# One load on another queue, three stores halved by columns, and a new order of visits in a seven-product weight gradient

## The chip, the cores and the metric

The kernel runs on one core of a Trainium2 chip. The time is device microseconds (us) of one execution. The engines are TensorE (PE in the profile, its weight loads PEld), VectorE (DVE), ScalarE (ACT), GpSimd (POOL) and SyncE (SP). SP and ACT issue plain DMAs, each on a queue of its own; POOL issues DMAs that also convert f32 to bf16. All of these queues are served by the same 16 DMA engines.

## The reference

```python
batch, m, k, n = 16, 512, 1024, 768          # f32
grad_weight = np.einsum('bmk,bmn->kn', input, grad_output)
return grad_weight.astype(np.float32)        # 1024 x 768
```

It is one matrix product: X (8192 x 1024) transposed, times G (8192 x 768). The sum runs over 8192 rows.

## The kernel before, in words

**Slices and pairs.** The 8192 rows are cut into 64 slices of 128 rows. Two slices make a unit u = 0 to 31. Units 0 to 4 and 31 are worked on as single slices ("s" in `LOADS`, L12): four result blocks A, B, C, D (K halves by N halves), each of four row blocks q of 128, get one matmul per slice. Units 5 to 30 are worked on as pairs ("P"): seven products (A, B, C, 1, 5, 6, 7) take the place of eight, in the manner of Strassen and Winograd. For them DVE makes sums and differences of the halves: `x0.u`, `x1.u`, `x2.u` of X (L195, L197, L199) and `g0.u`, `g1.u`, `g2.u` of G (L205, L207, L209). One block matmul is 128x128 weights against 384 columns.

**Loads.** Slice 0 of both inputs and X of slice 1 come as f32 (tiles `xf` and `gf`, L141 to L144): SP issues the left and then the right 384 columns of G, ACT issues X of slice 0 and then X of slice 1. DVE and ACT round these to bf16 in twelve pieces, `r0` to `r16` in the plan (L216 to L229): r10 and r11 are the left half of G, r0 the right half; r12 to r16 are X of slice 0; r1 to r4 are X of slice 1. Everything else is loaded by POOL straight into bf16: slices of units 0 to 4 one by one (L171, L173), later units whole (L166, L167), into ten buffers for each of X and G.

**Banks and visits.** PSUM has eight banks. A visit "C2@7.3" opens bank 7 for block C, q = 2, and adds three slices or pairs to it; "C2.1" goes on with an open one. Bank numbers 0 to 2 hold the four A blocks, packed, all along; two of these are cut over two banks and so take two matmuls a visit (128 and 256 columns). "c" and "v" close a visit on ACT or DVE: the first time by a copy, later by an add to the sum in SBUF (DVE, L364) or, where "f" had first filled the bank with the old sum (ACT, L292), by a copy back (ACT, L360). "z" puts a bank aside and "y" adds it later (L376, L385). At the end "v" adds a shared product (L357) or, for product 5, subtracts it from two sums (L352, L353), and "w" lets POOL do such an addition in SBUF (L392).

**What sets the order.** `PLAN` (L15 to L76) is a list of some 2,000 tokens written out. It is run through once (L394) and gives PE, DVE, ACT and POOL their instructions in exactly that order: each engine works its own off in order and waits where data, a bank or a buffer is late. POOL's loads stand ahead of its additions; SP's stores follow in the order in which blocks are closed. PE gets 920 block matmuls. `SPARE_LOADS` (L87) adds a second weight load to every other matmul in a range. The last block to close is B3, over two banks: its 256 columns leave by ACT's queue and its 128 by SP's (L366); every other block leaves by SP's (L370).

Of the kernel before, what the change touches and what calls it, by code (L numbers as in the profile page):

```python
# [9 lines left out]
P = 128  # L10
# [2 lines left out]


PLAN = (  # L15
    "r11 r10 r16 r14 r15 A1.1 r13 r12 A0.1 C2@7.1 C0@3.1 A2.1 A3.1 cC0 r0 vC2 D1@6.1 D3@5.1 r4 B2@4.1 r2 "
    "B1@7.1 vD1 r3 B0@3.2 cB2 A0.1 r1 B1.1 vD3 cB0 A2.1 A3.1 D0@6.1 cB1 D0.1 D2@3.2 cD0 D3@7.1 C3@5.2 vD3 "
    "C1@4.2 cC3 C1.1 A1.2 cC1 C0@5.2 cD2 A2.1 D1@4.2 C2@3.2 vD1 B3@7.3 vC2 B3.1 A3.2 vB3 D0@4.2 B1@6.2 vD0 "
    "B2@3.2 zcB1.0 B2.1 A2.1 A0.1 vB2 A0.1 D3@6.2 vC0 D3.1 C1@7.2 C3@5.2 vC1 C3.1 A1.2 vC3 A0.1 B0@3.2 vD3 "
    "B0.2 D2@7.2 vB0 D2.2 C2@5.1 fC3@3 A1.1 vD2 B3@4.2 A0.1 fD2@6 C3.1 vB3 C1@7.1 A2.1 cC3 A2.1 vC1 A0.1 A2.1 "  # L20
    "B3@4.1 D0@3.2 vB3 C2.3 B2@7.3 A3.2 vB2 A3.2 D2.1 vC2 D2.1 C0@7.5 B1@5.2 vC0 B1.2 A0.1 yB1.0 D1@7.6 B1.1 "
    "A0.1 A1.3 D0.3 D3@4.5 B1.1 D0.1 vD3 D2.2 D1.1 vD0 A3.1 cD2 A3.1 vB1 B0@4.1 zcD1.17 B0.2 g0.5 B0.1 B2@3.2 "
    "vB0 B2.1 B3@6.2 g1.5 B3.1 C1@5.1 vB2 C1.3 g2.5 C3@3.1 vB3 C3.3 x0.5 C3.1 C2@6.3 vC3 C2.1 52@4.1 C1.1 "
    "yD1.17 zcC2.5 A0.1 72@3.1 c52 A2.1 x1.5 A2.2 c72 A2.1 g0.6 62@7.1 vC1 A1.2 70@4.1 g1.6 50@3.1 63@5.1 c70 "
    "v62 73@6.1 A0.1 A3.1 g2.6 12@4.1 x2.5 C0@7.2 c12 C0.1 x0.6 C0.1 c50 A2.1 A3.1 f62@4 A0.1 x1.6 73.1 "
    "71@3.1 vC0 71.1 c73 63.1 A1.1 c71 x2.6 62.1 B3@7.1 c63 yC2.5 61@6.2 B3.1 c62 g0.7 B2@3.2 c61 60@5.2 vB2 "
    "B1@4.2 c60 B0@6.1 vB3 B0.1 10@3.2 vB0 11@5.2 g1.7 11.1 10.1 x0.7 13@6.1 c11 13.2 c10 A0.1 g2.7 53@5.1 "
    "vB1 53.1 fC1@3 53.1 70@7.1 x1.7 70.1 c13 A1.1 51@4.1 v70 c53 51.2 C1.1 g0.8 C1.1 c51 A3.1 x2.7 C3@5.1 "
    "cC1 C3.1 72@4.1 g1.8 72.1 vC3 f12@3 52@6.2 A2.1 g2.8 12.1 f71@5 12.1 x0.8 12.1 f60@7 A2.1 A0.1 A1.1 c12 "
    "x1.8 72.1 71.2 v72 f73@3 52.1 60.2 c71 x2.8 73.2 v52 c60 61@4.2 c73 A3.1 g0.9 63@7.1 fC0@5 63.1 v61 "  # L30
    "50@3.2 fB2@6 50.1 v63 C0.1 f10@4 C0.1 B2.1 g1.9 B2.1 B1@7.2 g2.9 cB2 10.1 x0.9 10.1 C0.1 C2@6.1 c10 C2.1 "
    "vB1 C2.2 f62@4 A2.1 x1.9 50.1 f51@7 A3.1 A0.1 x2.9 62.2 v50 62.1 51.1 vC2 51.1 c62 B0@3.2 g0.10 B0.1 "
    "fC1@4 B3@6.2 vB0 c51 B3.1 C1.2 vB3 A1.1 f70@3 13@7.2 x0.10 cC1 13.1 70.2 f11@6 A1.1 v13 70.1 A2.1 g1.10 "
    "11.1 f53@7 11.1 x1.10 11.1 A3.1 c70 g2.10 53.2 x2.10 c11 53.1 71@3.1 g0.11 71.1 c53 61@4.2 v71 B2@6.1 "
    "fC3@7 B2.1 A0.1 v61 60@3.2 vB2 C3.1 f12@4 C3.2 g1.11 C0.1 f63@6 12.1 x0.11 12.2 cC3 63.2 c12 x1.11 A0.1 "
    "A1.1 fB0@7 A3.1 x2.11 60.1 63.1 B0.1 v60 B0.1 c63 A2.1 72@4.1 g2.11 f73@3 72.1 g0.12 72.1 C0.1 cB0 "
    "B1@6.1 v72 B1.2 f10@7 73.1 g1.12 73.2 vB1 11@4.1 10.1 c73 10.1 g2.12 10.1 x0.12 f53@3 C0.1 11.1 50@6.1 "
    "c10 50.1 v11 50.1 53.1 f51@7 53.1 v50 C1@4.2 c53 C1.1 x1.12 A0.1 fB3@6 51.1 g0.13 51.2 52@3.1 vC1 52.1 "
    "c51 52.1 x2.12 52.1 A3.1 fC2@7 g1.13 A2.1 B3.1 v52 f70@4 B3.2 C2.1 g2.13 C2.1 fC3@3 C2.1 x0.13 C2.1 A1.2 "
    "cC2 70.1 x1.13 70.1 cB3 70.1 72@7.1 x2.13 72.1 c70 C3.2 v72 C3.1 61@6.2 g0.14 cC3 61.1 62@4.1 fB2@7 62.1 "  # L40
    "v61 62.2 fB1@3 B2.1 g1.14 B2.2 g2.14 B0@6.2 v62 cB2 A3.1 B1.1 vB0 B1.1 f11@7 C0.2 x0.14 cB1 12@4.3 11.1 "
    "f63@3 11.1 v12 71@6.3 x1.14 f60@4 71.1 63.1 x2.14 63.1 cC0 63.1 v71 A3.1 60.1 c63 60.1 g0.15 60.1 A2.2 "
    "c60 73@6.1 g1.15 73.2 g2.15 53@4.2 v73 13@3.4 f52@6 x0.15 13.1 11.1 zc53.20 C1@5.2 x1.15 c11 C1.1 51@4.2 "
    "vC1 51.1 A1.2 v13 fC2@5 A2.1 52.1 x2.15 52.2 g0.16 50@7.2 c52 50.1 C2.2 v50 B3@3.2 cC2 B3.1 v51 70@6.2 "
    "zcB3.6 g1.16 A0.2 f72@7 x0.16 A0.2 A1.1 A3.1 v70 A3.1 A2.1 72.1 x1.16 f70@6 72.2 x2.16 71@3.2 c72 y53.20 "
    "B0@5.3 v71 70.1 B1@7.2 c70 vB0 B1.1 10@3.1 f63@4 10.1 vB1 10.2 fB2@5 63.1 g0.17 63.1 f13@7 12@6.2 x0.17 "
    "12.1 c63 A3.1 13.2 v12 10.1 A1.1 A0.1 zc10.17 x1.17 B2.2 g2.16 B2.1 g1.17 73@3.2 cB2 g0.18 73.1 62@6.1 "
    "c13 62.1 v73 62.2 61@4.1 g1.18 61.1 fC0@3 61.1 g2.17 61.1 g2.18 f53@5 C3@7.2 v61 C3.2 C0.1 x0.18 C0.3 "
    "C3.1 v62 53.1 cC0 53.2 x1.18 53.1 51@3.1 vC3 51.1 c53 51.1 60@4.1 f50@6 g0.19 60.3 fC2@5 yB3.6 A0.1 A2.1 "
    "f11@7 A2.1 y10.17 A1.1 50.2 x2.18 50.1 C2.1 v60 C2.1 c50 C2.1 11.2 cC2 x0.19 11.2 52@4.2 c11 x1.19 52.2 "  # L50
    "x2.17 70@5.1 fB3@7 70.1 g1.19 70.1 A3.1 x2.19 A3.1 zc70.2 51.1 g0.20 A1.1 f72@6 B3.3 zc52.7 g1.20 B3.1 "
    "g2.19 72.2 cB3 v51 72.1 B1@4.2 c72 g2.20 B1.1 C1@5.2 vB1 C1.3 x0.20 53@7.1 71@3.2 vC1 71.2 A2.2 x1.20 "
    "f62@5 A1.1 53.1 x2.20 B2@4.2 v71 B2.2 B0@6.2 vB2 B0.2 62.1 g0.21 f73@4 62.2 v53 63@3.2 c62 63.1 g1.21 "
    "63.1 f13@7 A3.1 vB0 A3.1 A0.2 y70.2 A0.1 13.2 g2.21 13.1 x0.21 13.1 C0@6.2 c13 C0.1 73.1 x1.21 f61@5 "
    "73.3 x2.21 A2.1 61.1 vC0 c73 61.2 zc63.21 61.1 g0.22 60@6.1 f50@7 60.1 y63.21 60.1 12@4.2 zc60.4 g1.22 "
    "12.2 x0.22 12.1 A0.1 A1.2 v12 72@6.2 x1.22 72.1 50.1 y52.7 50.1 zc72.19 50.2 c61 g2.22 C2@4.1 B1@3.1 "
    "x2.22 51@6.1 f10@5 51.1 g0.23 51.1 C2.1 c50 C2.1 v51 C2.1 B1.2 g1.23 10.2 zcB1.2 g2.23 10.3 x0.23 10.1 "
    "70@7.2 c10 70.1 y72.19 70.1 52@3.2 v70 52.2 A3.1 vC2 A3.1 zc52.9 C3@6.1 x1.23 C3.1 f61@5 C3.2 x2.23 C3.1 "
    "A0.1 B3@4.1 vC3 B3.3 g0.24 61.2 vB3 11@7.2 c61 11.1 x0.24 11.1 fB0@4 11.1 A2.3 v11 71@5.2 x1.24 71.1 "
    "fB2@7 71.1 A0.1 x2.24 A1.1 B0.1 g0.25 B0.3 g1.24 A3.1 62@6.1 g1.25 cB0 62.1 g2.24 62.1 fC1@3 62.1 v71 "  # L60
    "B2.3 v62 B2.1 13@5.2 g2.25 cB2 13.1 x0.25 13.1 f63@6 53@4.4 x1.25 53.1 63.1 y60.4 63.3 v13 63.1 C0@7.2 "
    "g0.26 c63 C0.2 A1.1 f51@6 g1.26 C1.2 y52.9 C1.3 vC0 A0.1 51.1 cC1 51.2 zc53.12 12@5.1 x0.26 12.1 c51 "
    "12.2 A3.1 g2.26 A3.1 60@7.1 x1.26 60.2 v12 60.2 A1.1 yB1.2 A1.1 72@3.2 g0.27 72.2 v60 70@4.3 v72 73@5.1 "
    "f50@7 73.2 g1.27 73.1 f52@3 73.1 x2.26 10@6.2 g2.27 10.2 x0.27 50.3 v73 50.2 A1.1 v70 A2.1 c50 A2.2 "
    "x1.27 52.1 f61@7 52.1 g0.28 52.2 A0.2 g1.28 61.1 x2.25 61.2 x2.27 61.1 C0@5.1 v10 C0.1 c61 B3@4.2 c52 "
    "g2.28 B3.2 B2@6.1 x0.28 B2.2 C0.1 C2@7.1 vB2 C2.3 x1.28 C2.2 vC0 A0.1 A3.2 vB3 fB1@5 63@6.2 g0.29 63.1 "
    "A2.1 62@3.1 v63 62.3 x2.28 B1.1 fC3@6 B1.1 v62 B1.3 g1.29 B1.1 C3.1 g2.29 C3.2 x0.29 C3.3 A2.1 y53.12 "
    "13@4.1 cC3 13.2 x1.29 cB1 13.1 71@6.2 v13 71.3 g0.30 f10@4 C1@5.2 v71 C1.1 zcC2.3 C1.1 11@3.1 x2.29 11.1 "
    "f12@7 11.1 vC1 11.2 10.1 g1.30 12.1 f60@5 12.2 x0.30 12.1 f71@6 11.1 10.1 c12 10.1 v11 A2.1 A1.3 f61@7 "
    "x1.30 13@3.1 c10 A0.1 61.1 v13 61.2 71.1 x2.30 f62@3 60.2 v61 60.1 f72@4 60.1 62.1 v71 f63@7 62.1 72.2 "  # L70
    "g2.30 72.1 f53@6 72.1 v62 63.2 A3.1 v60 f73@3 A3.3 v72 fC0@5 A2.2 v63 73.3 vA3 73.1 f70@7 A1.2 v73 A0.3 "
    "vA2 70.1 f50@3 wC3 70.2 vA1 70.1 53.2 vA0 53.1 wC1 fC3@4 53.2 v70 C0.1 f52@0 C0.2 v53 C0.1 fC1@7 50.3 "
    "fD0@1 C3.2 vC0 C3.1 fB1@6 wD3 C1.2 v50 fD1@2 C1.1 D0.2 f51@5 52.1 wB3 52.1 cC1 52.1 yC2.3 D1.2 v52 51.1 "
    "fD3@7 51.2 cC3 51.2 fD2@3 D3.1 vD0 D3.1 B1.1 fC2@4 B1.1 v51 B1.1 cD3 B1.1 D2.2 C2.1 fB2@7 C2.1 vD2 C2.1 "
    "fB0@1 C2.1 B2.1 vB1 B2.1 fB3@3+0 B2.2 vD1 B2.1 B0.1 vC2 B0.3 vB2 B0.4 B3.2 vB0 B3.3 cB3 "
).split()  # L76


WARMUP = [("b", 512), ("f", 512), ("f", 512), ("b", 512)]
PAIRS_HELD = 10  # L80
SUMS_HELD = 8
ASIDE = 24

MERGED = 5


SPARE_LOADS = range(200, 450)  # L87
PACKED = True
PLACES = {
    0: [(0, 0, 0, 384)],  # L90
    1: [(0, 384, 0, 128), (1, 0, 128, 384)],
    2: [(1, 256, 0, 256), (2, 0, 256, 384)],
    3: [(2, 128, 0, 384)],
}


HALVED = 3


@with_exitstack  # L100
def kernel(
# [6 lines left out]
    nc = tc.nc  # L108
# [11 lines left out]
    X = input.rearrange("b m k -> (b m) k")  # L120
# [20 lines left out]
    nc.sync.dma_start(out=gf[:, LEFT], in_=G[0:P, LEFT])  # L141
    nc.scalar.dma_start(out=xf[0], in_=X[0:P, :])
    nc.sync.dma_start(out=gf[:, RIGHT], in_=G[0:P, RIGHT])
    nc.scalar.dma_start(out=xf[1], in_=X[P : 2 * P, :])  # L144

    wps = psum.tile([P, 512], f32, name="bank7")
    for dt, cols in WARMUP:
# [119 lines left out]
    fresh = {(p, q): True for p in streams for q in range(Q)}  # L267
    closed = set()
    opened = {}
    stored = []  # L270
    used = {7}

    def bank(b):
# [57 lines left out]
    def store(p, q, c0, c1, queue):  # L331
        row = q if p in "AB" else Q + q
        at = (0 if p in "AC" else NH) + c0
        halves = [slice(0, P)]
        if len(stored) < 2 * HALVED:
            halves = [slice(0, P // 2), slice(P // 2, P)]
        for rows in halves:
            stored.append(rows)
            queue.dma_start(out=OUT[rows, row, at : at + c1 - c0], in_=sum_of(p, q)[rows, c0:c1])

    def close(engine, p, q):
        parts, carried = opened.pop((p, q))
# [107 lines left out]
```

## Time and profile before

| | |
|---|---|
| runs shown | 162.37, 162.81, 163.12 us; median 162.81 |
| profiled execution | 162.31 us, its span 160.5 us, clock 1.00 |
| PE busy | 154.8 us, 1007 matmuls (6 of them warm-up) |
| DVE busy | 140.0 us, 323 instructions |
| ACT / POOL busy | 91.5 / 41.9 us |
| PE, first and last matmul of the product | starts at 5.22 us, ends at 156.69 us |
| last load lands / last store lands | 142.69 us / 159.62 us |
| DMA | 33.4 MB, mean 208 GB/s |

The page divides the span into 40 slices of 4 us and gives each engine's busy share in tenths. The timeline lists instructions in the order of time, like ones merged: start, time from the first one's start to the last one's end, engine, line, operation, count, and in brackets the idle time ahead of them and what ended it. A landing time is the moment at which the last of the 16 DMA engines told that its part is done; these times and the single packets are in the trace's DMA records.

### The profile page before, as it was taken

The page shows a single profiled execution, that of the slowest core. Times are in us where ns is not written, and L with a number is a line of the kernel's source. Part 1 is how long each engine was busy: PE and PEld are TensorE (multiplying, and loading weights), DVE is VectorE, ACT ScalarE, POOL GpSimd, SP SyncE. Part 2 cuts the span into 40 slices and gives each one's busy share as a digit, 9 for nine tenths or more (in the row PEclk, how much of TensorE's full clock was granted, in tenths as well). Part 3 has the DMA queues.
Part 4 walks back from the last instruction along what each step waited for, and adds up shares of the span by engine and source line. Part 5 has one row for each costly group of instructions (what it writes and reads, how often), then busy time and mean ns, then how long its engine had stood idle before and what let it go on. Part 6 is the DMA issues. An engine that isn't in the chain of part 4 may idle for free.

```text
span 160.5 us, 2979 instructions
## 1 busy us (share of the span) xinstructions
PE 154.8 (96%) x1007; PEld 99.8 (62%) x1132; DVE 140.0 (87%) x323; ACT 91.5 (57%) x206; POOL 41.9 (26%) x79
## 2 busy tenths in 40 slices
PE   8799999999999999999999999999999999999990
PEld 3266666577777766776665666666666656666560
DVE  0548853999999999999999989999999989999991
ACT  3571301167998888885675774654443423776940
POOL 7445433222212222221222221222222100004400
PEclk9999999999999999999999999999999999999999
DMA  4999999999999999999999999999999999932776
GB/s 168 298 206 210 208 210 216 212 215 213 211 213 213 213 213 212 213 214 215 214 213 212 212 213 212 214 212 212 214 214 212 213 213 214 212 60 67 229 259 231
DMA packets 13310, 33.41 MB, mean 208 GB/s; under 512 B 1520, under 2 KB 5104, under 8 KB 13296
## 3 DMA queue, kind: packets, MB, share of 16 engines
q0 software_dynamic: 10224, 28.64, 90.9%
q1 hardware_dynamic: 2640, 3.41, 6.6%
q10 hardware_dynamic: 432, 1.18, 1.9%
q8 instruction: 8, 0.13, 0.3%
q14 instruction: 6, 0.05, 0.1%
HBM read 58.72 MB, written 3.15 MB: 385 GB/s over the span
## 4 chain that ended last, share of the span: by engine, by line
PE 91%; DMA 3%; DVE 2%; issue 1%; SPq 0%; DVEq 0%
PE bank L321 91%; DMA gf<-in_grad_output_dram 3%; DVE acc L357 1%; DVE macc L353 0%; SPq L141 0%; DVE gp L213 0%; DVE bank L292 0%; DVE macc L352 0%; DVEq L445 0%; DVEq L357 0%; DVEq L362 0%
## 5 line engine op out<-in xcount | busy, mean ns | idle before, releaser
L321 PE MATMUL bank<-gp,xp 128*128 128x384 bf16 (+2 forms) x689 | 110.8, 307 | 1.1 <-DVE gp L213 0.7
L321 PEld LDWEIGHTS <-xp 128*128 128x128 bf16 x689 | 64.5, 98 | 32.8 <-DVE xp L213 1.5
L321 PE MATMUL bank<-ge,xe 128*128 128x384 bf16 x312 | 62.1, 326 | 0.0
L321 PEld LDWEIGHTS <-xe 128*128 128x128 bf16 x312 | 29.9, 97 | 14.2 <-DVE xe L197 0.3
L364 DVE TENSOR_TENSOR acc<-bank,acc 128x384 f32<-128x384 f32 x56 | 29.9, 552 | 9.1 <-PE bank L321 8.7
L360 ACT COPY macc<-bank 128x384 f32<-128x384 f32 x59 | 27.1, 481 | 14.3 <-PE bank L321 13.4
L292 ACT COPY bank<-macc 128x384 f32<-128x384 f32 x56 | 26.7, 484 | 11.3 <-DVE macc L364 6.0
L364 DVE TENSOR_TENSOR macc<-bank,macc 128x384 f32<-128x384 f32 x52 | 28.2, 553 | 0.9 <-PE bank L321 0.4
L360 ACT COPY acc<-bank 128x384 f32<-128x384 f32 (+1 forms) x35 | 16.2, 475 | 17.9 <-PE bank L321 17.6
L167 POOL DMA_DIRECT2D xp<-in_input_dram x27 | 14.3, 530 | 44.6 <-DMA xp<-in_input_dram 19.8
L166 POOL DMA_DIRECT2D gp<-in_grad_output_dram x27 | 14.3, 530 | 36.1 <-PE bank L321 23.6
L292 ACT COPY bank<-acc 128x384 f32<-128x384 f32 (+1 forms) x35 | 16.4, 482 | 9.4 <-DVE acc L364 6.3
L195 DVE TENSOR_TENSOR xe<-xp 128x1024 bf16<-128x1024 bf16 x26 | 17.8, 684 | 0.1
L205 DVE TENSOR_TENSOR ge<-gp 128x768 bf16<-128x768 bf16 x26 | 14.3, 550 | 0.0
L376 ACT COPY aside<-bank 128x384 f32<-128x384 f32 x15 | 7.2, 480 | 8.8 <-PE bank L321 8.6
L197 DVE TENSOR_TENSOR xe<-xe,xp 128x512 bf16<-128x512 bf16 x26 | 10.9, 419 | 0.3
L199 DVE TENSOR_TENSOR xp<-xp,xe 128x512 bf16<-128x512 bf16 x26 | 10.8, 420 | 0.3
L320 PEld LDWEIGHTS <-xp 128*128 128x128 bf16 x76 | 7.4, 98 | 4.6 <-DMA xp<-in_input_dram 0.3
L392 POOL TENSOR_TENSOR acc<-acc,macc 128x384 f32<-128x384 f32 x4 | 3.9, 1000 | 20.7 <-DVE macc L357 19.8
L209 DVE TENSOR_TENSOR gp<-ge,gp 128x384 bf16<-128x384 bf16 x26 | 9.1, 351 | 0.2
L207 DVE TENSOR_TENSOR ge<-gp,ge 128x384 bf16<-128x384 bf16 x26 | 9.0, 351 | 0.1
L320 PEld LDWEIGHTS <-xe 128*128 128x128 bf16 x49 | 4.8, 98 | 2.7
(24 smaller groups left out, 47.4 us busy)
## 6 DMA issues: line engine op xcount, KB each, us to landing
xp<-in_input_dram POOLq DMA_DIRECT2D x27, 512.0 KB, 16.7
gp<-in_grad_output_dram POOLq DMA_DIRECT2D x27, 384.0 KB, 16.7
out_dram<-acc SPq DMA_DIRECT2D x12, 192.0 KB, 2.0
xp<-in_input_dram POOLq DMA_DIRECT2D x8, 256.0 KB, 8.5
gp<-in_grad_output_dram POOLq DMA_DIRECT2D x9, 192.0 KB, 8.5
xf<-in_input_dram ACTq DMA_DIRECT2D x2, 512.0 KB, 5.0
out_dram<-acc SPq DMA_DIRECT2D x6, 96.0 KB, 2.2
gf<-in_grad_output_dram SPq DMA_DIRECT2D x2, 192.0 KB, 4.7
```

The costliest lines, as they stand in the source:

```text
L166: nc.gpsimd.dma_start(out=gp, in_=G[rows, :].rearrange("(p m) n -> p m n", m=2))
L167: nc.gpsimd.dma_start(out=xp, in_=X[rows, :].rearrange("(p m) k -> p m k", m=2))
L195: nc.vector.tensor_sub(out=xe[:, 0:2, :], in0=x[:, 1::-1, :], in1=x[:, 3::-2, :])
L197: nc.vector.tensor_sub(out=xe[:, 2, :], in0=xe[:, 0, :], in1=x[:, 0, :])
L199: nc.vector.tensor_add(out=x[:, 1, :], in0=x[:, 2, :], in1=xe[:, 2, :])
L205: nc.vector.tensor_add(out=ge[:, 0:2, :], in0=g[:, 0:2, :], in1=g[:, 1::2, :])
L209: nc.vector.tensor_add(out=g[:, 1, :], in0=ge[:, 2, :], in1=g[:, 2, :])
L292: copy(out=tile_[:, t0 : t0 + c1 - c0], in_=sum_of(p, q)[:, c0:c1])
L320: nc.tensor.ldweights(stat)
L321: nc.tensor.matmul(tile_[:, t0 : t0 + c1 - c0], stat, mov[:, c0:c1], start=start, stop=True, skip_group_check=True,)
L360: nc.scalar.copy(out=d, in_=b)
L364: nc.vector.tensor_add(out=d, in0=b, in1=d)
```

## The change

X of slice 1 is issued by SP behind the right half of G, instead of by ACT behind X of slice 0. Of the stores, number 0, 1 and 7 are cut into two halves of 192 columns with all 128 partitions; before, the first three were cut into two halves of 64 partitions. `PLAN` is another list: the same 920 block matmuls, the same roundings and sums, in another order, with 146 "v" for 137, 100 "c" for 94, 96 "f" for 91, 9 "z" and 9 "y" for 15 and 15, and 3 "w" for 4. Its last block takes banks 3 and 6 instead of 3 and 0. The range of spare weight loads ends five matmuls later.

```diff
 PLAN = (
-    "r11 r10 r16 r14 r15 A1.1 r13 r12 A0.1 C2@7.1 C0@3.1 A2.1 A3.1 cC0 r0 vC2 D1@6.1 D3@5.1 r4 B2@4.1 r2 "
-    "B1@7.1 vD1 r3 B0@3.2 cB2 A0.1 r1 B1.1 vD3 cB0 A2.1 A3.1 D0@6.1 cB1 D0.1 D2@3.2 cD0 D3@7.1 C3@5.2 vD3 "
...
-    "fD3@7 51.2 cC3 51.2 fD2@3 D3.1 vD0 D3.1 B1.1 fC2@4 B1.1 v51 B1.1 cD3 B1.1 D2.2 C2.1 fB2@7 C2.1 vD2 C2.1 "
-    "fB0@1 C2.1 B2.1 vB1 B2.1 fB3@3+0 B2.2 vD1 B2.1 B0.1 vC2 B0.3 vB2 B0.4 B3.2 vB0 B3.3 cB3 "
+    "r11 r10 r16 r14 A1.1 r13 C3@6.1 r0 r12 A2.1 r15 B3@7.1 cC3 B1@3.1 D0@5.1 cB3 A0.1 vB1 B2@4.1 cD0 A3.1 "
+    "D2@7.1 r1 C1@3.1 r3 r2 D1@6.1 vB2 r4 D3@5.2 D2.1 D1.1 cD3 B0@4.2 cD1 A3.1 C0@5.1 cB0 C0.1 C2@6.2 cD2 "
...
+    "C0.2 v50 fD1@5 C0.1 52.2 cC2 52.1 D1.1 fB2@6 D1.1 v52 B1.2 cD1 B1.1 B2.1 fD0@2 B2.1 vB1 B2.2 fD2@0 B2.1 "
+    "vC0 D0.1 fB0@5 D0.1 D2.1 vB2 D2.1 B0.2 vD2 B0.1 fB3@3+6 B0.2 vD0 B0.2 B3.2 vB0 B3.3 cB3 "
 ).split()
...
-SPARE_LOADS = range(200, 450)
+SPARE_LOADS = range(200, 455)
...
-HALVED = 3
+HALVED = (0, 1, 7)
...
     nc.sync.dma_start(out=gf[:, RIGHT], in_=G[0:P, RIGHT])
-    nc.scalar.dma_start(out=xf[1], in_=X[P : 2 * P, :])
+    nc.sync.dma_start(out=xf[1], in_=X[P : 2 * P, :])
...
-        halves = [slice(0, P)]
-        if len(stored) < 2 * HALVED:
-            halves = [slice(0, P // 2), slice(P // 2, P)]
-        for rows in halves:
-            stored.append(rows)
-            queue.dma_start(out=OUT[rows, row, at : at + c1 - c0], in_=sum_of(p, q)[rows, c0:c1])
+        cuts = [c0, (c0 + c1) // 2, c1] if stored[0] in HALVED else [c0, c1]
+        stored[0] += 1
+        for a, b in zip(cuts, cuts[1:]):
+            queue.dma_start(out=OUT[:, row, at + a - c0 : at + b - c0], in_=sum_of(p, q)[:, a:b])
```

## The prediction

> **What bounds the kernel now.** I read the page first, then the chain of waits, the timeline of the head, of the middle and of the tail, and the busy time by stage.
>
> ```profile
> span 160.5 us, 2979 instructions
> PE 154.8 (96%) x1007; PEld 99.8 (62%) x1132; DVE 140.0 (87%) x323; ACT 91.5 (57%) x206; POOL 41.9 (26%) x79
> PE   8799999999999999999999999999999999999990
> DVE  0548853999999999999999989999999989999991
> ```
>
> PE is full from the second slice to the last but one, and the chain of waits gives it 91% of the span. DVE is full too, but from the eighth slice on only. The steady pace of PE comes from a merged row of the timeline, 18 matmuls of 384 columns in 2.93 us: 0.1625 us each; a visit that is cut over two banks takes 0.1655 (starts 0.056 and 0.1095 apart). All 920 make 149.73 us, in either order. From the first (5.22) to the end of the last (156.69) are 151.47 us, so PE lost 1.75 us in all. This is the whole account that an order can improve in the stream; the rest is head and tail. The head:
>
> ```profile
> 4.91 0.56 DVE L213 CAST xp<-xf 128x128 bf16<-128x128 f32 x3
> 5.22 1.30 PE L321 MATMUL bank<-gp,xp 128*128 128x128 bf16 x8 [0.41 <-DVE xp L213]
> 6.79 0.36 DVE L213 CAST gp<-gf 128x384 bf16<-128x384 f32 x1 [1.32 <-DMA gf<-in_grad_output_dram]
> 7.10 0.71 ACT L213 CAST xp<-xf 128x256 bf16<-128x256 f32 x2 [0.39 <-DMA xf<-in_input_dram]
> 7.21 0.97 PE L321 MATMUL bank<-gp,xp 128*128 128x384 bf16 x5 [0.69 <-DVE gp L213]
> ```
>
> Six visits, then PE waits for r0, the right half of G. By matmul starts (6.20 to 7.21, less one matmul) that is 0.85 us; 0.15 more went before it. DMA landings of the two halves of G:
>
> ```profile
> L141 SPq DMA_DIRECT2D gf<-in_grad_output_dram x1: 378/378/378, 0.7 to 0.7; - x1
> ...
> DMA to landing us min/median/max: 3.8/3.8/3.8
> L143 SPq DMA_DIRECT2D gf<-in_grad_output_dram x1: 421/421/421, 1.2 to 1.2; - x1
> ...
> DMA to landing us min/median/max: 5.6/5.6/5.6
> ```
>
> Same size, but the second (landed 6.77) shared the DMA engines with X of slice 1 (landed 7.08), and its last three packets with POOL's first load. In the middle the loads set the pace:
>
> ```profile
> 56.78 0.69 DVE L195 TENSOR_TENSOR xe<-xp 128x1024 bf16<-128x1024 bf16 x1
> 56.80 0.10 PEld L320 LDWEIGHTS <-xp 128*128 128x128 bf16 x1 [0.17 <-DMA xp<-in_input_dram]
> 57.98 0.10 PEld L321 LDWEIGHTS <-xe 128*128 128x128 bf16 x1 [0.29 <-DVE xe L197]
> ```
>
> X of unit 11 landed at 56.757, 4.8 us after that of unit 10, where the others follow by 4.3: the DMA records show a 16 KB packet of instructions at 54.75 that held one engine for 0.98 us. Of the 0.63 us that PE lost after the head, 0.36 fell by 58.5, most of it here. The tail:
>
> ```profile
> 149.18 1.96 POOL L392 TENSOR_TENSOR acc<-acc,macc 128x384 f32<-128x384 f32 x2 [0.95 <-DVE macc L353]
> 150.41 1.15 DVE L385 TENSOR_TENSOR acc<-acc,aside 128x384 f32<-128x384 f32 x1
> 151.64 5.05 PE L321 MATMUL bank<-gp,xp 128*128 128x384 bf16 x35
> 154.93 1.93 DVE L357 TENSOR_TENSOR acc<-bank,macc 128x384 f32<-128x384 f32 x4
> 156.62 0.37 ACT L360 COPY acc<-bank 128x256 f32<-128x256 f32 x1 [1.80 <-PE bank L321]
> 156.79 0.28 DVE L362 COPY acc<-bank 128x128 f32<-128x128 f32 x1
> ```
>
> With E the end of PE (156.69): ACT's store of B3 lands at E+2.73, SP's at E+2.93, and the span ends 0.9 later.
>
> **The change part by part.** *X of slice 1 on SP.* ACT's queue loses one issue (0.46 us at 1.17); ACT then waits for G until 4.59 anyway: nothing. SP issues it behind both halves of G, 0.46 us from about 1.60; SP has nothing else before the stores: nothing. On the DMA engines the right half of G now meets only X of slice 0, whose last packets end at 4.47. By 4.5 half of it (92 of 192 KB) had gone already in the profile; the other half, four packets an engine at 0.065 us, takes 0.3 us alone: data by 4.8 to 4.9, landing 0.35 to 0.4 later as for the others: 5.2. Bounds: 5.0 (at once with X of slice 0, 4.89) and 6.77 (no change). I take 5.2, nearest to the row of X of slice 0. X of slice 1 has the same bytes ahead of it; alternating with POOL's packets (0.157 against 0.134 us) it lands at 7.1 to 7.7; I take 7.2.
>
> *The head of the order.* Now r0 is third on DVE, ahead of r12 and r15, which queue behind its wait. Start-to-start: r0 5.2, r12 5.5, r15 5.65. PE: A1 5.22, C3 5.40, A2 5.69 (r13 ends 5.62 on ACT), B3 5.86 (r0 done 5.56), and then without a wait to slice 1's first matmul, due at 7.33 + 0.2 = 7.5; r3 (0.40 from 7.22) lets it go at 7.7. One more bank (vB2 behind r1 and r2 on DVE, 8.2) and PE has lost 0.4 us where it had lost 1.0: a gain of 0.6 at this point (0.3 to 0.75).
>
> *What the loads leave of it.* The loads' bytes, order and saturation stay, so landings stay. Ahead of the first use of X of unit 9 stand 41.68 us of PE work in both orders, and it landed at 47.63: PE must have lost 0.78 by then. Ahead of unit 11 stand 50.47 in both: 1.12 lost; its product 6 comes after 51.61 (51.45 before) and waits for x0 and x1 (57.93): 1.16 lost, where it was 1.32. So of the 0.6 gained only 0.2 is left behind unit 11, if that load is late again; the instruction fetch comes with the same matmul, some 0.3 earlier, inside the same transfer. After unit 11 no landing asks for over 0.8. Later stalls were 0.26 (banks and g2.12); I keep 0.1 to 0.26, since the shortest work between a bank's last matmul and its next use is nearly the same (0.81 us at least before; one of 0.65, all others 0.81, after). PE loses 1.3 to 1.4: E comes 0.35 to 0.45 earlier. If unit 11 were on time: 0.78 + 0.2 lost, 0.8 earlier.
>
> *More evictions.* DVE has three instructions more (nine "v", six "y" less), at 0.466 start to start 1.4 us; ACT's eleven "c" and "f" for six "z" hide in its 43% idle time, or cost up to 0.4 each where PE waits. From the first pair sum on DVE has 292 for 291 instructions, 121.1 us, beside 126.8 us of PE work where it was 120.7 beside 127.8: its spare time shrinks by 1.45 us. Busy time by stage:
>
> ```profile
> 30.00:60.00 30.00, 30.00 (x202) 21.30 (x283) 29.58 (x69) 23.42 (x55) 7.42 (x14) 1.00 1.07 213
> 90.00:120.00 30.00, 30.00 (x201) 18.67 (x199) 28.99 (x69) 16.11 (x36) 7.42 (x14) 1.00 1.07 213
> ```
>
> (PE, PEld, DVE, ACT, POOL.) DVE is idle 0.4 to 1.1 us in 30, 3.2 between 30 and 150. Cost: 0 if the work falls into these gaps, 1.45 if none does. I take 0: its sums by the order leave it at most as late as before.
>
> *Tail.* Before, DVE's add from aside took 1.15 us instead of 0.55 beside POOL's addition and left DVE late: B0's add ended at E+0.17, SP issued B0 (0.42 us) and only then B3's last columns, at E+0.74. In the new order no "y" stands behind the first "w", and the last adds are ready at E-4.7 (C0), -2.6, -2.0, -2.3 and -0.8 (B0): B0's ends at E-0.2, SP is free at E+0.3, B3's columns go at E+0.42. SP's landing comes 0.32 earlier, ACT's stays at E+2.73 and is last: 0.2 gained (0 to 0.35). POOL has one addition less (1.0 us), off the path.
>
> *Halves by columns.* Twenty stores as before, 0.33 to 0.6 us each on SP, whatever their shape; eight follow number 7's halves, and SP waited 4.8 us in all for data: nothing, up to 0.3 if that slack were gone. Three spare weight loads (0.1 each) lie beside matmuls: nothing.
>
> **Sum.** 0.4 + 0.2 = 0.6 off 162.31: 161.7 for an execution like the profiled one. That one was 0.5 below the median of the runs, 162.81, so I state 162.2 for the median. 0.5% (0.81 us) is about what can be told from no change here.
>
> **Rivals.**
> *Loads do not bind* (0.20). The instruction fetch hits another load, or unit 11 is on time: E 0.8 earlier, tail 0.2: 161.8. For it: the other landings ask for 0.8 only. Against: the fetch is bound to PE's instructions.
> *G does not come earlier* (0.11). Then r0 holds DVE until 6.79 and PE has three visits done instead of six: lost 1.5 by 7.21. But the loads ask for 1.16 later anyway, so with 0.26 more it ends at 1.76 as before: only the tail's 0.2 is left, 162.6. The Trainium skill ("DMA: Bandwidth & Descriptors", "Issuing engines are not separate DMA queues") speaks for this: by it, issuing from several engines saves issue time alone, so that moving a load to another engine would not change the transfers. The two halves of G, 3.8 and 5.6 us, rather show that what stands in the other queue matters.
> *DVE becomes the bound* (0.13). DVE is the engine nearest to full; the 1.45 us of lost slack show up as late evictions behind 36 us: 162.81 - 0.2 + 1.45 = 164.1. It decides once over 0.8 us of it find no gap, with PE waiting on DVE sums and adds. Against: before, DVE kept up at 97%.
>
> **How the numbers follow.** The forecast has 0.56: 162.2, on its own 161.7 to 162.8. Range: from the first rival less 0.6 of spread between runs to two thirds of the way to the last: 161.2 to 163.6. Faster by over 0.5% (under 162.0): most of the first rival and a little of the forecast, 0.22; slower: the last and a little, 0.14; within: 0.64.
>
> **What would show it.** Right half of G landing near 5.2 and PE without a gap from 5.7 to 7.5; PE waiting for X of units 7 to 9 and 11 where it hardly did; E near 156.3; SP's last store issued at E+0.4. Wrong: G at 6.8; PE waiting on DVE adds in mid-stream; landings of all loads moved as a whole, which I hold fixed.

## The result

| | before | after |
|---|---|---|
| median of 18 runs each, us | 162.84 (162.04 to 163.15) | 163.23 (162.85 to 163.72) |
| profiled execution / its span, us | 162.31 / 160.5 | 163.65 / 161.9 |
| first product matmul starts / last ends (E), us | 5.22 / 156.69 | 5.23 / 158.47 |
| right half of G / X of slice 1 landed, us | 6.77 / 7.08 | 5.23 / 8.36 |
| last store landed | E+2.93 | E+2.50 |

The changed kernel takes 1.0031 times as long, 95% interval 1.0018 to 1.0044: 0.3% slower, where a small gain was forecast. The time lies between the prediction's bounds (161.2 and 163.6), and the move is under the 0.5% that it could tell from no change, but the sign is wrong. The two profiled executions stand on opposite sides of their medians (0.5 below, 0.4 above), so their 1.34 us is more than the change is worth: some 0.4 between the medians.

The page of the kernel after hardly differs from that of before. DVE has 0.8 us more of work, PE is as full:

```profile
span 161.9 us, 2984 instructions
PE 155.3 (96%) x1007; PEld 99.4 (61%) x1134; DVE 140.8 (87%) x326; ACT 92.9 (57%) x211; POOL 41.2 (25%) x78
PE   8789999999999999999999999999999999999991
DVE  0427766998899999999999899999999999989991
PE 82%; DMA 12%; POOL 1%; DVE 1%; issue 1%; ACT 1%; ACTq 0%; POOLq 0%
```

The last line, the chain of waits (the work that ended last, followed back), has moved: a DMA now holds 12%. Told in order of time (start, length, what), the chain after names three places:

```profile
12.55 10.24 DMA xp<-in_input_dram
22.80 0.04 issue
22.84 15.17 PE bank L322 x104
38.02 0.01 issue
38.03 0.57 DVE macc L363
...
38.64 50.87 PE bank L322 x332
...
90.61 0.57 DVE macc L363
91.18 0.04 issue
91.22 67.26 PE bank L322 x444
```

A load at 22.8, and two single DVE sums of 0.57 us at 38.03 and 90.61. To size them I took, as for the prediction, each matmul's start less the one before and less its own steady duration, and summed these losses of PE by stretch:

| PE lost, us | to 9.2 | 9.2-36 | 36-53 | 53-64 | 64-88 | 88-100 | from 100 | all |
|---|---|---|---|---|---|---|---|---|
| before | 1.00 | 0 | 0.06 | 0.42 | 0.04 | 0 | 0.05 | 1.57 |
| after | 1.56 | 0.43 | 0.55 | 0.07 | 0.10 | 0.38 | 0.25 | 3.33 |

(The prediction's 1.75 for before counts to the modelled end of the last matmul and with gaps between the first ones; the table is matmul starts alone, so that kernels can be compared.) The head, in the timeline after (start, length, engine, line, operation, and in brackets idle time and what ended it):

```profile
5.23 2.29 PE L322 MATMUL bank<-gp,xp 128*128 128x128 bf16 x15 [0.39 <-DVE xp L214]
5.25 0.36 DVE L214 CAST gp<-gf 128x384 bf16<-128x384 f32 x1
8.38 0.71 ACT L214 CAST xp<-xf 128x256 bf16<-128x256 f32 x2 [1.37 <-DMA xf<-in_input_dram]
8.38 0.51 DVE L214 CAST xp<-xf 128x256 bf16<-128x256 f32 x2 [1.56 <-DMA xf<-in_input_dram]
8.84 0.88 PE L322 MATMUL bank<-gp,xp 128*128 128x384 bf16 x4 [1.32 <-ACT xp L214]
```

The right half of G is there at 5.25 and PE runs through all of slice 0 without the old wait. Then it stands still for X of slice 1, which landed at 8.355, 1.3 us later than before. The issue itself is as expected, 0.43 us at 1.6; the transfer is not (the view of the load's line):

```profile
L145 SPq DMA_DIRECT2D xf<-in_input_dram x1: 432/432/432, 1.6 to 1.6; - x1
...
DMA to landing us min/median/max: 6.7/6.7/6.7
```

At 22 us PE waits for X of slice 7:

```profile
22.84 0.83 PE L322 MATMUL bank<-gp,xp 128*128 128x384 bf16 x5 [0.24 <-DMA xp<-in_input_dram]
```

The DMA records show a 16 KB packet of instructions at 20.75 that held one DMA engine for 0.94 us while this load was under way. The load landed at 22.80; the loads ahead of it came 2.2 us apart, so that it was due at some 21.07. In the middle, DVE's timeline:

```profile
37.21 0.42 DVE L200 TENSOR_TENSOR xp<-xp,xe 128x512 bf16<-128x512 bf16 x1
38.03 0.56 DVE L363 TENSOR_TENSOR macc<-bank,macc 128x384 f32<-128x384 f32 x1 [0.39 <-PE bank L322]
38.50 0.55 DVE L206 TENSOR_TENSOR ge<-gp 128x768 bf16<-128x768 bf16 x1
```

The bracket puts the 0.39 us of idle time down to PE. But the semaphore instruction with which DVE waits for PE (a "bare wait" below: an instruction that only waits, ahead of the sum) had ended at 37.58, and the sum started 0.45 later. The same happens at 90.61 (wait over at 90.20) and 144.05 (143.66):

```profile
89.69 0.42 DVE L200 TENSOR_TENSOR xp<-xp,xe 128x512 bf16<-128x512 bf16 x1
90.61 0.56 DVE L363 TENSOR_TENSOR macc<-bank,macc 128x384 f32<-128x384 f32 x1 [0.49 <-ACT acc L359]
...
143.46 0.42 DVE L200 TENSOR_TENSOR xp<-xp,xe 128x512 bf16<-128x512 bf16 x1
144.05 1.49 DVE L356 TENSOR_TENSOR macc<-bank,macc 128x384 f32<-128x384 f32 x3 [0.18 <-issue]
```

Each of these sums also has a wait of its own on ACT; the first experiment shows that it was not this one that held them. Counted over all of DVE's instructions in the trace, semaphore instructions included and from 0, these sums are numbers 63, 191 and 319: 128 apart.

Last, the tail after:

```profile
155.17 1.97 DVE L356 TENSOR_TENSOR acc<-bank,macc 128x384 f32<-128x384 f32 x4
157.24 1.07 DVE L356 TENSOR_TENSOR acc<-bank,macc 128x384 f32<-128x384 f32 x2
158.51 0.29 DVE L361 COPY acc<-bank 128x128 f32<-128x128 f32 x1 [0.20 <-PE bank L322]
```

No add is stretched beside POOL any more, SP issued its last store at E+0.39 (before E+0.74), and the last landing is 0.4 closer to E.

So after the result there were three candidates for the loss: X of slice 1 on SP's queue (0.56 us in the head), a load delayed by a packet of instructions (0.4), and three late starts of DVE (PE lost 1.07 more than before in their three stretches).

### The profile page after: what moved, and what is told of

The parts are those of the page before. It is cut to its first block, busy times and chain, and to the rows that moved or that the text cites. A ratio compares the mean times of both kernels' runs of the same rounds, so it can differ in the third digit from the quotient of the medians.

```text
span 161.9 us, 2984 instructions
## 1 busy us (share of the span) xinstructions
PE 155.3 (96%) x1007; PEld 99.4 (61%) x1134; DVE 140.8 (87%) x326; ACT 92.9 (57%) x211; POOL 41.2 (25%) x78
## 4 chain that ended last, share of the span: by engine, by line
PE 82%; DMA 12%; POOL 1%; DVE 1%; issue 1%; ACT 1%; ACTq 0%; POOLq 0%
PE bank L322 82%; DMA xp<-in_input_dram 12%; POOL gp L172 1%; DVE macc L363 1%; ACT acc L359 1%; POOL xp L174 0%; DVE acc L361 0%; ACTq L359 0%; POOLq L433 0%
## 5 line engine op out<-in xcount | busy, mean ns | idle before, releaser
L322 PE MATMUL bank<-gp,xp 128*128 128x384 bf16 (+2 forms) x689 | 112.7, 307 | 2.3 <-ACT xp L214 1.3
L322 PE MATMUL bank<-ge,xe 128*128 128x384 bf16 x312 | 63.8, 326 | 0.1
L293 ACT COPY bank<-macc 128x384 f32<-128x384 f32 x59 | 28.2, 483 | 16.9 <-DVE macc L363 10.4
L363 DVE TENSOR_TENSOR acc<-bank,acc 128x384 f32<-128x384 f32 x62 | 32.6, 552 | 4.9 <-PE bank L322 4.6
L359 ACT COPY macc<-bank 128x384 f32<-128x384 f32 x63 | 29.0, 482 | 13.6 <-PE bank L322 13.0
L363 DVE TENSOR_TENSOR macc<-bank,macc 128x384 f32<-128x384 f32 x56 | 30.3, 552 | 1.8 <-PE bank L322 1.2
L293 ACT COPY bank<-acc 128x384 f32<-128x384 f32 (+1 forms) x37 | 17.6, 482 | 20.1 <-DVE acc L363 16.3
L359 ACT COPY acc<-bank 128x384 f32<-128x384 f32 (+1 forms) x37 | 16.9, 477 | 8.2 <-PE bank L322 7.7
L391 POOL TENSOR_TENSOR acc<-acc,macc 128x384 f32<-128x384 f32 x3 | 3.0, 1000 | 21.8 <-DVE macc L356 20.5
L356 DVE TENSOR_TENSOR acc<-bank,macc 128x384 f32<-128x384 f32 (+2 forms) x15 | 6.8, 498 | 0.0
```

The source lines that it names most:

```text
L293: copy(out=tile_[:, t0 : t0 + c1 - c0], in_=sum_of(p, q)[:, c0:c1])
L322: nc.tensor.matmul(tile_[:, t0 : t0 + c1 - c0], stat, mov[:, c0:c1], start=start, stop=True, skip_group_check=True,)
L359: nc.scalar.copy(out=d, in_=b)
L363: nc.vector.tensor_add(out=d, in0=b, in1=d)
```

## The experiments

**Moving DVE's count by two.** The three late starts could belong to these sums, or to their place in the count. Two tiny instructions of DVE at the start move every later one by two places.

```diff
     x0, x1, g0 = items[0][1], items[1][1], items[0][2]
+    pad = accp.tile([P, 1], f32, name="pad")
+    for _ in range(2):
+        nc.vector.memset(pad, 0.0)
```

> The changed kernel with two one-column memsets more at the head of VectorE, where it is idle. All later instructions of VectorE move two places on in its program. In the trace of the changed kernel VectorE starts its 63rd, 191st and 319th instruction about 0.4 us late, with nothing to wait for; these are 128 apart. Theory that a boundary in the instruction stream costs VectorE 0.4 us where it falls behind a bare semaphore wait: the three gaps vanish (the boundary now falls on an x2 sum that waits for x1 anyway), TensorE loses about 1.0 us less (0.55 at 38 us, 0.35 at 91, 0.2 at 145), time 162.2 to 162.6. Theory that the order itself is late there (a late ScalarE copy, a full bank): the gaps stay at the same instructions, time 163.2.

Measured: 162.42 us (162.06 to 162.66), ratio to before 0.9972 (0.9959 to 0.9985): work was added, and the kernel is faster than both. The sum behind the same wait starts on time:

```profile
36.53 0.42 DVE L200 TENSOR_TENSOR xp<-xp,xe 128x512 bf16<-128x512 bf16 x1
36.95 0.56 DVE L366 TENSOR_TENSOR macc<-bank,macc 128x384 f32<-128x384 f32 x1
37.42 0.55 DVE L206 TENSOR_TENSOR ge<-gp 128x768 bf16<-128x768 bf16 x1
```

All three are gone; numbers 63, 191 and 319 are now sums `x2`, and start 0.035 us or less behind the end of the one ahead. PE's losses in the stretches 36 to 53, 88 to 100 and from 100 fall from 0.55, 0.38, 0.25 to 0.15, 0.02, 0.06: 0.95 us. The two ratios to before, 0.9972 and 1.0031, are 0.96 us apart. The late starts cost this kernel more than its whole loss. The run also settles the wait on ACT. The last copies of ACT that ended ahead of the first two late sums ended at 37.87 and 90.44; with the two memsets the same sums start at 36.95 and 89.17, before these same copies end (37.20 and 89.37), so they do not wait for them. Ahead of the third, ACT's last had ended 0.67 us before.

**X of slice 1 back on ACT's queue.** The changed kernel, with one line as before.

```diff
-    nc.sync.dma_start(out=xf[1], in_=X[P : 2 * P, :])
+    nc.scalar.dma_start(out=xf[1], in_=X[P : 2 * P, :])
```

> The changed kernel with X of slice 1 back on ScalarE's queue: the new order and stores alone. Theory that the move of the load costs (X of slice 1 lands at 8.36 instead of 7.08, all of GpSimd's loads 0.31 later): X of slice 1 lands at 7.1 again, the loads 0.3 earlier, the right half of G at 6.8; TensorE has lost 1.5 us by 7.3, hardly anything more for slice 1, so about as much as the changed kernel's 1.5 at the head, and 0.3 less behind late loads: 162.8 to 163.2. Rival, that the load's move has no part in the result: 163.2. Had the move paid: 163.6 or more.

Measured: 162.90 us, ratio 1.0018 (0.9997 to 1.0038). X of slice 1 landed at 7.04 and the right half of G at 5.95 (6.8 was expected), and PE lost 0.69 us in the head where the changed kernel lost 1.56. The three late starts stayed (37.24, 89.82, 143.28), and X of slice 7 was again late (22.01, a packet of instructions at 19.93; PE lost 0.49). So the late starts have nothing to do with the load's queue.

**The load moved alone.** The kernel before, with X of slice 1 on SP.

```diff
-    nc.scalar.dma_start(out=xf[1], in_=X[P : 2 * P, :])
+    nc.sync.dma_start(out=xf[1], in_=X[P : 2 * P, :])
```

> The kernel before with the load of X of slice 1 moved to SyncE's queue and nothing else. Theory that the move delays X of slice 1 by 1.3 us and all of GpSimd's loads by 0.3: the right half of G lands at 5.2, the wait for it goes, TensorE stops for X of slice 1 instead, some 1.7 us lost by 8.8 where it was 1.0; 163.2 to 163.7. Rival, that the move is good and the order is what costs: below 162.6.

Measured: 162.93 us, ratio 1.0008 (0.9997 to 1.0019), below the 163.2 to 163.7 expected. The right half of G landed at 5.41, X of slice 1 at 8.40, and PE lost 1.73 us in the head instead of 1.00. In the trace that is 0.7 worse, in the medians 0.1, which is inside the noise: for the kernel before, no cost of the load's move is shown. The landings repeat from kernel to kernel; what they cost does so only roughly.

**Halves by rows.** The changed kernel with its first three stores cut into 64 partitions each, as before.

```diff
-        cuts = [c0, (c0 + c1) // 2, c1] if stored[0] in HALVED else [c0, c1]
-        stored[0] += 1
-        for a, b in zip(cuts, cuts[1:]):
-            queue.dma_start(out=OUT[:, row, at + a - c0 : at + b - c0], in_=sum_of(p, q)[:, a:b])
+        halves = [slice(0, P)]
+        if len(stored) < 2 * HALVED:
+            halves = [slice(0, P // 2), slice(P // 2, P)]
+        for rows in halves:
+            stored.append(rows)
+            queue.dma_start(out=OUT[rows, row, at : at + c1 - c0], in_=sum_of(p, q)[rows, c0:c1])
```

> The changed kernel with the first three stores halved by rows as before. All theories of the load and of the order expect no difference from the changed kernel, 163.2 within 0.15; if the halves by columns matter, the first four stores of SyncE take another time each (0.35 to 0.44 us by columns) and the end moves by 0.1 to 0.3.

Measured: 163.14 us, ratio 1.0027 (1.0011 to 1.0042): no difference from the changed kernel. SP's first six issues took 0.47 to 0.60 us each by rows, and 0.33 to 0.44 in the changed kernel, where four of the six are halves by columns and two are whole; but the last store still issued at E+0.39. This part is worth nothing here. X of slice 7 was on time in this execution (PE lost 0.06 from 9.2 to 36), and the three late starts were there.

**Two places and the load on ACT.** The first experiment with the second's line.

```diff
-    nc.sync.dma_start(out=xf[1], in_=X[P : 2 * P, :])
+    nc.scalar.dma_start(out=xf[1], in_=X[P : 2 * P, :])
...
+    pad = accp.tile([P, 1], f32, name="pad")
+    for _ in range(2):
+        nc.vector.memset(pad, 0.0)
```

> The changed kernel with VectorE's program moved on by two memsets and X of slice 1 back on ScalarE's queue. With the three late instructions gone, TensorE lost 1.73 us in the kernel with the two memsets alone, 1.32 of it at the head; with the load on ScalarE's queue the head lost 0.69. Theory that the loads leave little of a gain at the head (they ask for 0.8 to 1.2 us lost by 57 us): 0.4 to 0.5 us of waits for loads come up at 20 to 57 us instead, time 0 to 0.25 below the 162.42 of the kernel with the memsets alone. Theory that the head's gain reaches the end: 0.6 below it, 161.8.

Measured: 161.96 us (161.83 to 162.00), ratio 0.9957 (0.9940 to 0.9975), the lowest time of the study. PE lost 0.91 us in the head (1.32 with the load on SP), but a packet of instructions at 20.0 made X of slice 7 late once more (0.31 lost). The gain over the first experiment, 0.46, lies between the two expectations, and the intervals of the two overlap: that the load is better off on ACT is shown by the landings and PE's waits, and by the ratios only made likely.

```profile
5.21 1.14 PE L325 MATMUL bank<-gp,xp 128*128 128x128 bf16 x5
6.59 2.62 PE L325 MATMUL bank<-gp,xp 128*128 128x384 bf16 x15 [0.24 <-DVE gp L214]
```

PE's rows in this kernel's timeline: one short wait for the right half of G (landed 6.15), and none for slice 1, against the 1.32 us wait above.

**The load cut in two.** X of slice 1 in halves of columns, the upper behind G on SP, the lower on ACT, with the two memsets.

```diff
-    nc.sync.dma_start(out=xf[1], in_=X[P : 2 * P, :])
+    nc.sync.dma_start(out=xf[1][:, KH:K], in_=X[P : 2 * P, KH:K])
+    nc.scalar.dma_start(out=xf[1][:, 0:KH], in_=X[P : 2 * P, 0:KH])
```

> As the kernel with the two memsets, but X of slice 1 in two halves of columns: the upper half on SyncE's queue behind G, the lower half on ScalarE's behind X of slice 0. Both queues then have work until about 6.5 us. Theory that GpSimd's first load takes its share from X of slice 1 as soon as one of the two queues has run dry (at 4.4 us with the load on SyncE's queue alone, at 5.4 before): it starts later here, X of slice 1 lands at 6.7 to 7.1, the right half of G at 5.5 to 6.0, the head loses 0.5 to 0.8; time as for the load on ScalarE's queue, 162.1 to 162.4. Rival, that only the queue's length counts: X of slice 1 at 7.5 or later, time as with the memsets alone.

Measured: 162.77 us, ratio 1.0007 (0.9993 to 1.0020): a miss. ACT's half landed at 6.32, but SP's at 8.27, hardly earlier than the whole load, though it has half the bytes. The packets show when: the half's first packet went out at 5.65, though it was issued at 1.6, and POOL's had begun at 5.17. The half also has as many packets as the whole load, 128, each of 2 KB instead of 4. The time misses for another reason too: the span ends 1.34 us behind the last landing where it ends 0.91 behind it in the first experiment, because after that landing SP still goes through eight closing semaphore instructions instead of one. These 0.43 us are more than the 0.35 between the two medians, so what the split itself costs or gains does not show in the time.

**A first control.** If the count matters, late starts should be made in the kernel before too. Here 28 memsets bring a sum `x0` behind a bare wait (a semaphore instruction ahead of it) to place 191.

```diff
+    pad = accp.tile([P, 1], f32, name="pad")
+    for _ in range(28):
+        nc.vector.memset(pad, 0.0)
```

> The kernel before with 28 one-column memsets at the idle head of VectorE: its 163rd instruction, the x0 sum at 78.6 us, which stands behind a bare semaphore wait, becomes its 191st. Theory that the boundary in the instruction stream costs 0.4 us behind such a wait: this sum, which followed the wait after 0.06 us, now starts about 0.4 us later, TensorE loses 0 to 0.4 us after it, time 0 to 0.25% more than before. Rival, that the late starts belong to the new order's own instructions: no gap there, no change.

Measured: 162.89 us, ratio 1.0011 (0.9996 to 1.0025), and no late start:

```profile
79.21 0.35 DVE L207 TENSOR_TENSOR ge<-gp,ge 128x384 bf16<-128x384 bf16 x1
79.48 0.69 DVE L195 TENSOR_TENSOR xe<-xp 128x1024 bf16<-128x1024 bf16 x1
```

Place 190 was the wait (over at 79.44), place 191 the sum, 0.04 us after it and 0.27 us behind the start of the one ahead, its usual pace. A bare wait ahead is not enough, at least for this sum, which works on X and not on a bank. My next guess was that DVE must also have run empty in the wait.

**Three more shifts.** Two put a chosen sum, in whose wait DVE had stood idle, at place 191 or 319; a shift by one puts the waits themselves at 63, 191 and 319.

```diff
+    pad = accp.tile([P, 1], f32, name="pad")
+    for _ in range(26):
+        nc.vector.memset(pad, 0.0)
...
+    later = 7
     for token in PLAN:
...
+        if token == "vB2" and later:
+            for _ in range(later):
+                nc.vector.memset(pad, 0.0)
+            later = 0
```

This is the changed kernel with 33; the kernel before gets 26 and 9, behind "vC2"; the shift by one is the first diff with `range(1)`.

> The changed kernel with 33 one-column memsets of DVE added before its 16th microsecond, 26 at the start (0.125 us each, so done by 4.1 us, before the first rounding) and 7 behind the first sum of B2. They move DVE's instruction 158, a product's sum behind a bare wait (77.00 us, where it started 0.045 us after that wait), to the place of instruction 191. Theory (every 128th instruction of DVE can start about 0.4 us late, and does so behind a bare wait that DVE was standing idle in): that sum starts 0.35 to 0.45 us after its wait, the late starts at 38.0, 90.6 and 144.1 are gone, and PE loses 0 to 0.4 us at this one place: 162.4 to 162.9. Rival (the three late starts belong to those sums and their neighbours, and the two memsets only moved something else): no late start near 76 to 77 us, and either the three old ones are still there (163.2) or none is (162.4).

Measured: 162.30 us (6 runs), ratio 0.9972 (0.9952 to 0.9992). The late starts at 38, 90 and 144 are gone. But the control missed its mark: the trace has only 32 instructions of DVE more, a semaphore instruction having gone elsewhere, so the chosen sum stood at 190, on time; 191 was the sum right behind it, with DVE busy, also on time. On the place itself it says nothing.

> The kernel before with 35 one-column memsets of DVE, 26 at the start and 9 behind the first sum of C2. They move DVE's instruction 284, a sum behind a bare wait in which DVE had stood idle for 0.37 us (131.09 us, started 0.045 us after the wait), to the place of instruction 319. Theory (every 128th instruction can start late, where DVE stood idle in the wait ahead of it; the earlier control failed since DVE was not idle there): the sum starts 0.35 to 0.45 us after its wait, PE loses 0 to 0.4 us there, 162.8 to 163.3. Rival (the late starts belong to the changed kernel's order, not to the count of instructions): 0.045 us as before, and the time of the kernel before.

Measured: 162.77 us, ratio 1.0004 (0.9992 to 1.0016), and the late start is there. DVE's rows in the kernel before, and then with 35 memsets:

```profile
129.99 0.69 DVE L195 TENSOR_TENSOR xe<-xp 128x1024 bf16<-128x1024 bf16 x1
131.09 0.56 DVE L364 TENSOR_TENSOR acc<-bank,acc 128x384 f32<-128x384 f32 x1 [0.41 <-PE bank L321]
```

```profile
130.25 0.68 DVE L195 TENSOR_TENSOR xe<-xp 128x1024 bf16<-128x1024 bf16 x1
131.70 0.56 DVE L367 TENSOR_TENSOR acc<-bank,acc 128x384 f32<-128x384 f32 x1 [0.77 <-PE bank L324]
```

Same sum, same wait, over 0.37 us after the instruction ahead in both. At place 284 the sum starts 0.045 us behind the wait, at place 319 it starts 0.396 behind it. PE lost 0.22 us from 100 us on instead of 0.05.

> The changed kernel with one one-column memset of DVE ahead of its roundings, so that each bare wait itself stands at places 63, 191 and 319 and the sum behind it one further. Theory one (the first instruction of a block of 128 is the late one, whatever it is): the wait's own record comes 0 to 0.4 us late, and where PE's sums had been ready by then the sum behind it is late with it; 162.6 to 163.2. Theory two (what counts is that the late one stands behind a wait; the fetch of the wait itself runs beside the work of the instruction ahead): the late starts are gone, as with two memsets; 162.4.

Measured: 162.20 us (4 runs), ratio 0.9962 (0.9947 to 0.9977). Theory two: with the waits themselves at 63, 191 and 319 nothing is late; the sums behind start 0.04 to 0.08 us after the wait.

**Does DVE have to be empty?** Two last shifts choose sums whose wait was over while DVE was still at work: 26 memsets at the start of the changed kernel, and 39 in the kernel before (26 at the start, 6 behind "vC2", 7 behind "vB2").

> The changed kernel with 26 memsets of DVE at the start. They bring DVE's instruction 165, a product's sum behind a bare wait (79.68 us in the profile of after, 0.12 us after the wait was over, since the instruction ahead ran on for 0.205 us more), to place 191. Theory one (any sum behind a bare wait is late at such a place, to 0.39 to 0.46 us after the wait, as at 144.05 us, where DVE was busy for 0.22 us more too): 0.39 to 0.46 us after the wait here, the three old late starts gone. Theory two (DVE must have run empty): 0.12 us, as before. Either way some 162.3 to 162.7 us, since the old late starts are gone.

Measured: 162.48 us, ratio 0.9987 (0.9971 to 1.0004). The three old late starts are gone and a new one is there, at the chosen place. DVE's rows with 26 memsets:

```profile
77.72 1.02 DVE L366 TENSOR_TENSOR macc<-bank,macc 128x384 f32<-128x384 f32 x2
78.94 0.56 DVE L366 TENSOR_TENSOR macc<-bank,macc 128x384 f32<-128x384 f32 x1 [0.21 <-ACT acc L362]
```

In the kernel after, the same three sums stand in one row, without a gap:

```profile
78.74 1.48 DVE L363 TENSOR_TENSOR macc<-bank,macc 128x384 f32<-128x384 f32 x3
```

The wait was over at 78.53, DVE worked on until 78.73, and the sum began at 78.94: 0.42 after the wait. It was not the copy of ACT in the bracket, which ended at 78.82: in the kernel after, the sum starts at 79.68, before that same copy ends (79.85). PE lost 0.29 us at 80.07. So DVE need not be empty; theory one comes out here, though not its word "any", which the first control contradicts, and work ahead only hides part of the 0.4.

> The kernel before with 39 memsets of DVE (26 at the start, 6 behind the first sum of C2, 7 behind the first of B2). They bring DVE's instruction 152, a product's sum from a bank behind a bare wait (73.74 us, 0.045 us after the wait, the instruction ahead running on for 0.11 us more), to place 191. In the failed control the same was so of a sum of X that waits for a load (0.126 us more of work ahead). Theory one (any sum from a bank is late there; the failed control differs by its kind of instruction): 0.39 to 0.46 us after the wait. Theory two (DVE must have run empty): 0.045 us. The time 162.8 to 163.3 by either.

Measured: 162.95 us, ratio 1.0010 (0.9995 to 1.0025). Off the mark again: the count moved by 38, the chosen sum stood at 190 and started 0.045 us after its wait. It tells nothing on the two theories.

**What the runs settle.** The late start follows the place in DVE's count and not the sum: it was taken away by 1, 2, 26 and 33 memsets, and made at two chosen places, one in either kernel. In the fourteen profiles I read, the numbers 63, 191 and 319, 42 in all. Thirteen of them are an instruction right behind a bare wait. Eleven of these began 0.39 to 0.46 us after the wait; one, with 26 memsets at 24.21, also did (0.44), but at its usual pace behind 0.5 us of work; the thirteenth is the failed control. The other 29 show no such start. Nor does any other place: of some 500 other sums and roundings behind a bare wait in these profiles, up to 158 us, none started over 0.25 us after the wait with DVE idle ahead of it for over 0.1 us, but for those that had a second wait on PE of their own.

What sets the failed control apart can be seen in the DMA records. Six packets of instructions of 8 KB fall into every span, three of which go with these numbers: in the failed control the packet came 0.9 us ahead of number 191; in the eleven late starts it came 0.65 to 3.35 us after. So the late start may go with a block of instructions that was not asked for ahead of time. That reading was made after the fact, and no run was aimed at it. The failed control differs in its kind too: its sum reads X in SBUF and waits for a load, while all that started late read a bank. No run here tells these two apart.

## Why the prediction was wrong

*The right half of G at 5.2: right.* It landed at 5.23, and at 5.16 to 5.41 in the other kernels with the whole of X of slice 1 behind it on SP; with that load on ACT it landed at 5.95 to 6.82. The rival "G does not come earlier" falls. Read as the prediction read it, the rule from the Trainium skill that stood beside it ("DMA: Bandwidth & Descriptors", "Issuing engines are not separate DMA queues") would have left the landing where it was; here the trace disagrees.

*X of slice 1 at 7.2, with bounds 7.1 to 7.7: wrong, the step that failed in the head.* It landed at 7.78 to 8.40 in all seven kernels that have it whole on SP, and at 7.01 to 7.28 in the six with it on ACT. I had let its packets follow G's at once and alternate with POOL's from the time when POOL's began before, 5.39. In the records POOL's packets began at 4.46, just after ACT's queue had sent its last (4.39), and those of X of slice 1 only at 5.05, after the last of G's (4.89). Before, both queues of SP and ACT had work until past 6, POOL's began at 5.39, and X of slice 1 moved from 4.31 to 6.60. So the load began 0.74 us later, and took 2.85 us instead of 2.29 beside POOL's packets: together about the 1.28 by which it landed later. In all seven kernels with the load on SP POOL's packets began at 4.34 to 4.55, in the six with it on ACT at 5.27 to 5.39. That they wait until one of the two queues runs dry is read from these times; the split, which was to test it, put them off to 5.17, and SP's half was late all the same. Price: the head's loss became 1.56 us instead of 0.4, and rose with the landing from kernel to kernel (1.24 at 7.78, 1.32 at 8.04, 1.41 at 8.19, 1.56 at 8.36).

*"Landings stay": wrong by 0.3 in the profile of after.* POOL's loads landed 0.25 to 0.54 later there, but for three: X of slice 7 (2.04 later), X of unit 11, which had been late before (0.01 earlier), and one load of G (0.1 earlier). That is no fixed price: with the load on SP, POOL's first landed at 7.19 to 7.98, with it on ACT at 7.45 to 7.74. Unit 11 landed at 56.75 and held nobody up, because PE was by then late through other causes: what the prediction let the loads take of the head's gain was not put to the test, as there was no gain.

*The instruction fetch inside unit 11's transfer: right in kind, wrong in place.* The packet that came at 54.75 before came at 56.97, not 0.3 earlier, and unit 11 had landed. In the profile of after another packet fell on X of slice 7 and PE lost 0.41 us; in three of the other thirteen profiles such a packet did the same, in ten it did not. The kernel with halves by rows, the same program up to the stores, was spared, so a hit is a matter of the single execution. This one is as large as what the profiled time has above the median.

*More evictions on DVE cost 0: wrong, the step with the largest price.* What failed is the reason given, that by their order DVE's sums would be at most as late as before. The added work itself was hidden, as argued; three of DVE's instructions were late by their place in the count, and PE waited for them: 0.95 us. The rival "DVE becomes the bound" named the engine and the sign (PE waiting for DVE's adds in mid-stream), and a price half as large again (1.45), but not the mechanism: moving these sums by two places, by adding work to DVE, gave all of it back.

*Tail: right in kind, twice as large.* SP's last store at E+0.39 (predicted E+0.42), its landing at E+2.50. ACT's landing was to stay last at E+2.73; it came at E+2.34, so 0.4 was gained, not 0.2; what let it land earlier is open.

*Halves by columns: nothing, right*, though not because shape makes no difference to the issue: a half by columns was issued in 0.33 to 0.44 us, one by rows in 0.47 to 0.60. (SP waited 4.1 us for data between its stores, not 4.8: the view's list gives 4.8 only with 0.7 at the start. Nothing rests on it.)

The sum: the changed order without its late starts is 0.28% faster than before (0.15 to 0.41), some 0.46 us of the 0.6 predicted. By the profiles of the two that is the tail (0.4), since its head is worse (1.32 us lost for 1.00); so the size is near by luck, with the parts shifted. The load on SP takes 0.1 to 0.5 by the medians, not clear of the noise in any one pair, and the late starts take the 0.96 that turn a gain into a loss. That 163.23 still lies under the upper bound is no merit either: the bound was worked out for another mechanism. (Two thirds of the way from 162.2 to the last rival would make it 163.5.)

## What to carry to other kernels

When an order is searched for or changed, look in the trace for single instructions that start some 0.4 us after all their waits are met, count their places on their engine, and where they are a fixed number apart, shift the whole engine by one or two cheap instructions and measure again: here that was worth more than the change. Before a load is put behind another on one queue to let a third come first, ask when it can itself begin, which queue runs dry through it, and whose packets come in between. Among several causes, size each by undoing it alone and comparing medians: the one trace of the changed kernel held a hit of 0.4 us that a kernel with the same start was spared, and stood 0.4 above its own median.

## What the runs showed of the hardware

- DVE's instructions number 63, 191 and 319 can start 0.4 us late behind a bare wait. 8 KB for 128 instructions would be 64 bytes for one; that blocks of this size are what is counted is inferred from the spacing and the packets. In the profile of after no such packet comes between the start and 38.03, and the next is at 41.36, so the late start is not the wait for that packet's arrival; what takes the 0.4 us stays open. The Trainium skill ("Runtime: NRT & Kernel Launch", "Instruction fetch mechanics") gives blocks of 256 instructions and 16 KiB, with the fetch hidden by the pace of dispatch; the spacing of 128 here disagrees with that for DVE, and so do the 0.4 us, if they are the fetch's.
- A third load behind two others on SP's queue, issued at 1.6, sent its first packet only at 4.50 to 5.05 in seven kernels, and at 5.65 where it was half as large. The half landed at 8.27, the whole at 7.78 to 8.40.
- A 16 KB packet of instructions held one DMA engine for 0.88 to 1.45 us (0.89 to 0.98 at the one near 20 us). In the four profiles in which X of slice 7 was late, it landed 2.02 to 2.10 us behind the start of that packet, 1.4 to 1.7 later than due (22.80 for 21.07 in the profile of after). Why the other ten, with that packet from 0.6 us before the landing to 0.2 after it, were spared is open.
